# Layer-1 MLP of a two-layer decoder step: product 6 combined in PSUM, the small tokens' last products one step earlier

## The chip, the core and the metric

The kernel runs on one core of one Trainium2 chip. The metric is the device time of one execution in microseconds (us). The engines are named as the profile names them: PE (TensorE, matmuls), DVE (VectorE), ACT (ScalarE), POOL (GpSimd) and SP (the sync engine, whose queue issues most DMAs; POOL's queue issues those that add to what is already in a buffer). PSUM is where matmuls accumulate; one bank holds 128 x 512 fp32.

## The reference, cut to what matters

Each of two layers is a mixer and an MLP, with a layer norm behind each. The change lies in the MLP of layer 1, the last stage of the program. D_MODEL is 1024, D_FF 4096; there are 1024 prompt tokens, and 8 sample tokens (the "small tokens") that pass through the same weights.

```python
def post_norm(x, f, g, b):
    return layer_norm(DEEPNORM_ALPHA * x + f, g, b)

def sq_relu_mlp(x, w1, w2):
    h = jax.nn.relu(x @ w1)
    return (h * h) @ w2
...
        x_p = post_norm(x_p, sq_relu_mlp(x_p, mlp_w1[layer], mlp_w2[layer]), ln_mlp_g[layer], ln_mlp_b[layer])
        x_s = post_norm(x_s, sq_relu_mlp(x_s, mlp_w1[layer], mlp_w2[layer]), ln_mlp_g[layer], ln_mlp_b[layer])
    y_prompt = x_p[:, N_META:]
```

## The kernel before

`mlp1()` runs the hidden width in four groups (g = 0 to 3) of 1024. In a group, x times a 1024 x 1024 block of w1 (the "up" half) and the hidden block times a 1024 x 1024 block of w2 (the "down" half) are each done as 2 x 2 blocks with seven products instead of eight. The seven are numbered i = 1 to 7 and run in the order 1, 2, 5, 6, 4, 3, 7 (up) and 1, 5, 6, 3, 7, 4, 2 (down), in the last group 1, 5, 6, 7, 4, 3, 2. Their operands are sums and differences of quarter blocks, by the tables `UP_W`, `UP_X`, `DOWN_H`, `DOWN_W`.

**One product.** An operand is split into a high and a low part (`split` for what is on the chip: ACT casts in L202, DVE subtracts in L203; `weight_operand` for weights: ACT casts in L1621, POOL subtracts in L1622). `mm3` makes three matmuls (L206 to L208). A tile is 12 matmuls into one PSUM bank: eight tiles of 128 x 258 in an up product (512 prompt columns and 4 small-token columns for each half of the tokens), four of 128 x 512 in a down product. Tiles take banks in turn, three named `axt` and three named `mmt`, so a bank is wanted again six tiles later.

**After a tile.** `up_tile` adds the tile into the four result blocks c11, c12, c21, c22 of `HF`. In product 6 it makes c21 = tile - c12 (L1667, PSUM in, SBUF out) and then c22 = c22 + c21 (L1666, all SBUF); product 4 later adds its tile to c21. `hidden` applies the squared ReLU (L1655, L1656) and copies the small tokens' columns to `hs` (L1657). `chip_operand` also forms sums of blocks on DVE (L1596, into `RX`).

**Loads.** SP loads weights into a pool of five buffers `rw`, two buffers `raw`, and a four-part buffer `RW` for running sums (L1618); POOL's queue adds second terms to them by DMA (L1620). A load waits in SP's queue until its buffer is free, and all that is behind it waits too.

**The small tokens' down product.** `beside` makes four matmuls of 32 rows (L1642) into the accumulators `acc` for each quarter of w2, placed after the first tile of a chosen product. Where the product's own weights are that plain quarter, its buffers are used; otherwise four further loads are made (L1628), and their four `rw` buffers are held until those matmuls. In the last group these stand in down products 1 (plain), 5, 6 and 7.

**The end.** After down product 7 of the last group `samples_out` copies `acc` (L1559), transposes (L1564), reduces and normalizes the small tokens on DVE, with two matmuls between (L748, L754), transposes back (L1573) and writes `y_sample` (L1576). `normalize` and `last` finish each prompt tile: `bn_stats` (L1076), the root by POOL's pow (L1085), scaling, and the output, for tiles 2 and 3 by L1549 to L1551 at the very end, for the others by L1096, L1544 and an adding DMA (L1545) onto the bias rows that L1760 has put into `y_prompt` (3 MB).

A scheduler orders the instructions of each engine from the program's order; engines run their own instructions strictly in that order, and wait for each other by semaphores.

Of the kernel before, what the change touches and what calls it, by code (L numbers as in the profile page):

```python
# [21 lines left out]
P = 128  # L22
# [5 lines left out]
TS = 32  # L28
# [79 lines left out]
UP_W = {1: [(0, 0)], 2: [(0, 1)], 5: [(1, 0), (1, 1)], 6: ["run", (0, 0)], 4: [(1, 1)], 3: ["run", (0, 1)], 7: [(0, 0), (1, 0), "new"]}  # L108
UP_X = {1: [(0, 0)], 2: [(1, 0)], 5: [(0, 1), (0, 0)], 6: [(1, 1), "run"], 4: [(1, 0), "run"], 3: [(1, 1)], 7: [(0, 1), (1, 1)]}
DOWN_H = {1: [(0, 0)], 2: [(0, 1)], 5: [(1, 0), (1, 1)], 6: [(0, 0), "run"], 3: [(0, 1), "run"], 4: [(1, 1)], 7: [(1, 0), (0, 0)]}  # L110
DOWN_W = {1: [(0, 0)], 2: [(1, 0)], 5: [(0, 0), (0, 1)], 6: ["run", (1, 1)], 4: ["run", (1, 0)], 3: [(1, 1)], 7: [(1, 1), (0, 1), "new"]}
# [3 lines left out]
def hybrid_step(ctx, tc, A, dbg=None, upto=9):  # L115
    nc = tc.nc
    V, S, G, TE = nc.vector, nc.scalar, nc.gpsimd, nc.tensor
    dma = nc.sync.dma_start
# [224 lines left out]
    ps = smt()  # L343
# [16 lines left out]
    ps = smt()  # L360
# [202 lines left out]
    ps = smt()  # L563
# [4 lines left out]
    ps = smt()  # L568
# [8 lines left out]
    ps = smt()  # L577
# [15 lines left out]
    ps = smt()  # L593
# [20 lines left out]
    ps = smt()  # L614
# [986 lines left out]
    def weight_operand(terms, quarter, side=None):  # L1601

        hi, lo = (wsp.tile([P, 2048], F32R, name=n).rearrange("p (k n) -> p k n", n=512) for n in ("whi", "wlo"))
        run = terms[0] == "run"
        own = []

        def src(q, k):
            w, r0, c0 = quarter(*q)
            return w[r0 + k * P : r0 + (k + 1) * P, c0 : c0 + 512]

        for k in range(4):
            if run or (len(terms) > 1 and terms[-1] != "new"):
                t = RW[:, k, :]
            else:
                count[1] += 1
                t = wrp.tile([P, 512], F32, name="raw") if count[1] % 7 in (0, 3) else rawt()
            if not run:
                loads.append(dma(t, src(terms[0], k)).ins)  # L1618
            if len(terms) > 1:
                nc.gpsimd.dma_start(t, src(terms[1], k), accum_op=ALU.add)  # L1620
            S.copy(hi[:, k, :], t)  # L1621
            G.tensor_tensor(lo[:, k, :], t, hi[:, k, :].bitcast(F32), op=ALU.subtract)  # L1622
            own.append(t)
        if side:
            if terms != [side.quarter]:
                own = [rawt() for k in range(4)]
                for k in range(4):
                    dma(own[k], src(side.quarter, k))  # L1628
            sides.append((side, own))
        return hi, lo  # L1630

    w1, w2 = A["mlp_w1"][1], A["mlp_w2"][1]

    def operands(g, up, i):
        if up:
            left = weight_operand(UP_W[i], lambda h, k: (w1, 512 * k, 1024 * g + 512 * h))
            right = chip_operand(UP_X[i], lambda k, c: xr(c)[:, 4 * k : 4 * k + 4, :], TH, RX)
            return left, right

        def beside(k, t):  # L1640
            r, u = beside.quarter
            TE.matmul(acc[u][k * TS : (k + 1) * TS, :], hs[:, 4 * r + k, :], t, start=g == 0 and i in (1, 3), stop=g == 3 and r == 1)  # L1642


        beside.quarter = ({1: (0, 0), 3: (1, 1), 7: (0, 1), 2: (1, 0)} if g < 3 else {1: (0, 0), 5: (0, 1), 6: (1, 0), 7: (1, 1)}).get(i)
        left = chip_operand(DOWN_H[i], lambda c, k: HF[:, 4 * k : 4 * k + 4, c, :512], 512, XF[0][:, : 4 * TH] if g == 3 and i == 7 else RX)
        right = weight_operand(DOWN_W[i], lambda k, u: (w2, 1024 * g + 512 * k, 512 * u), beside if beside.quarter else None)
        return left, right

    ups = []  # L1650
# [8 lines left out]
    def up_tile(g, i, m, c, left, right, ps):  # L1659
        (ah, al), (bh, bl) = left, right  # L1660
        ps = ps[:, :CH]
        ms, cs = slice(m * P, (m + 1) * P), slice(c * CH, (c + 1) * CH)
        for k in range(4):
            mm3(ps, ah[:, k, ms], al[:, k, ms], bh[:, k, cs], bl[:, k, cs], k == 0, k == 3)
        c11, c12, c21, c22 = (HF[:, 4 * h + m, x, cs] for h in range(2) for x in range(2))
        add = lambda out, x, y: ups.append(V.tensor_tensor(out, x, y, op=ALU.add).ins)  # L1666
        less = lambda out, x, y: V.tensor_tensor(out, x, y, op=ALU.subtract)  # L1667
        if i == 1:
            S.copy(c12, ps)
        elif i == 2:  # L1670
            add(c11, c12, ps)
        elif i == 5:
            S.copy(c22, ps)
        elif i == 6:
            less(c21, ps, c12)
            add(c22, c22, c21)
        elif i == 4:
            add(c21, c21, ps)
        elif i == 3:
            less(c12, ps, c22)  # L1680
        else:
            add(c22, c22, ps)
            add(c21, c21, ps)
        if c:
            for h, x in {2: [(0, 0)], 3: [(0, 1)], 7: [(1, 1), (1, 0)]}.get(i, ()):
                hidden(h, x, m)
# [23 lines left out]
    def mlp1():  # L1710
# [6 lines left out]
        for at, (g, up, i) in enumerate(seq):  # L1717
# [14 lines left out]
            for t in range(4):  # L1732
                if t == 2:
                    nxt = operands(*seq[at + 1])
                if t == 1 and sides:
                    side, own = sides.pop(0)
                    for k in reversed(range(4)):
                        side(k, own[k])
                if up:
                    for c in range(2):  # L1740
# [9 lines left out]
                if g == 3:  # L1750
                    for c, u in {7: [(1, 1)], 4: [(1, 0)]}.get(i, ()):
                        yield 4 * c + t, u
            if g == 3 and not up and i == 7:
                samples_out()
            if g == 3 and up and i == 7:
                for x, nm in ((fg, "g"), (fb, "b")):
# [36 lines left out]
```

## Time and profile before

| | us |
|---|---|
| median of 3 runs | 2802.86 (2800.35 to 2804.12) |
| the profiled execution | 2807.25 |
| its span | 2805.4 |
| PE busy | 2725.4 (97%) |
| DVE busy | 1935.9 (69%) |
| ACT busy | 1107.1 (39%) |
| POOL busy | 1091.0 (39%) |

The span is from the first to the last instruction; 1.85 us of the profiled execution's time lie around it. PE is busy nearly throughout, so what counts is where it is not, and what is left after its last matmul. Times in the trace are from the span's start. The MLP of layer 1 is what runs from about 2110 us on.

### The profile page before, as it was taken

Reading aid. Unit: us, or ns where it says so; the run is one execution under the profiler, and the core shown is the slowest. Engines: PE = TensorE matmul, PEld = TensorE weight load, DVE = VectorE, ACT = ScalarE, POOL = GpSimd, SP = SyncE. Lnnn points to the kernel's source line nnn. Section 1 sums busy time; section 2 is a strip of 40 time slices with the busy share of each in tenths; the row PEclk is TensorE's granted clock in tenths of the full one; section 3 lists DMA queues with packets and bytes.
Section 4 is the critical chain, followed back from the end, with each engine's and each line's share of the span. In section 5 each row is a group of like instructions: output and inputs, shape, how many; then the busy total and the mean of one; then the engine's idle time right before and its main releaser. Section 6 shows DMA issues by size and latency. Waiting matters only on the chain.

```text
span 2805.4 us, 52242 instructions
## 1 busy us (share of the span) xinstructions
PE 2725.4 (97%) x19849; PEld 2237.5 (80%) x19849; DVE 1935.9 (69%) x3011; ACT 1107.1 (39%) x2266; POOL 1091.0 (39%) x744
## 2 busy tenths in 40 slices
PE   8989999999999999999999999899999999999997
PEld 5867767987777777777798989777899889798985
DVE  5375363678787787777667730887647888978698
ACT  4324463152221222221242112777526546355553
POOL 2132112234344443434234312200026667686765
PEclk9999999999999999999999999999999999999999
DMA  7475545735798898888658995212044555564674
GB/s 237 164 242 207 202 154 184 262 97 184 284 333 320 310 351 302 331 319 306 250 173 312 363 368 169 64 55 79 31 126 90 103 139 113 134 133 104 140 179 112
DMA packets 275624, 562.81 MB, mean 201 GB/s; under 512 B 23510, under 2 KB 144412, under 8 KB 271276
## 3 DMA queue, kind: packets, MB, share of 16 engines
q1 hardware_dynamic: 256076, 522.75, 54.0%
q0 software_dynamic: 19296, 36.71, 8.1%
q8 instruction: 156, 2.56, 0.4%
q14 instruction: 96, 0.79, 0.1%
HBM read 533.00 MB, written 29.52 MB: 201 GB/s over the span
## 4 chain that ended last, share of the span: by engine, by line
PE 78%; DVE 9%; DMA 4%; ACT 4%; issue 3%; POOL 1%; SPq 0%; DVEq 0%; POOLq 0%; ACTq 0%
PE mmt L206 18%; PE mmt L207 18%; PE mmt L208 18%; PE smt L983 4%; PE axt L206 3%; PE axt L208 3%; PE axt L207 3%; PE smt L1359 2%; ACT as L1337 1%; DMA swt<-in_mlp_w 1%; DVE pg L942 1%; PE prt L1333 1%; PE axt L1354 1%; DVE XH L203 1%; DVE sc L943 1%
## 5 line engine op out<-in xcount | busy, mean ns | idle before, releaser
L194 POOL TENSOR_TENSOR wlo<-raw,whi 128x512 fp32r<-128x512 f32 x252 | 361.5, 1448 | 719.0 <-ACT whi L193 616.2
L206 PE MATMUL mmt<-whi,XH 128*128 128x256 f32 (+1 forms) x1760 | 524.2, 300 | 1.1 <-DVE ast L1335 0.9
L207 PE MATMUL mmt<-wlo,XH 128*128 128x256 f32 (+1 forms) x1760 | 522.8, 298 | 0.6 <-POOL wlo L194 0.6
L206 PE MATMUL mmt<-XH,whi 128*128 128x512 f32 (+1 forms) x1216 | 435.9, 360 | 3.4 <-DVE HL L203 1.8
L208 PE MATMUL mmt<-whi,XL 128*128 128x256 f32 x1536 | 432.6, 285 | 0.0
L208 PE MATMUL mmt<-XH,wlo 128*128 128x512 f32 (+1 forms) x1216 | 432.4, 356 | 0.2 <-POOL wlo L1622 0.2
L193 ACT CAST whi<-raw 128x512 fp32r<-128x512 f32 x252 | 150.4, 619 | 574.2 <-DMA raw<-in_mlp_w 172.9
L206 PEld LDWEIGHTS mmt<-whi,XH 128*128 128x128 f32 x1760 | 330.8, 189 | 39.6 <-issue 24.3
L943 DVE TENSOR_REDUCE sc<-pg 128x16 f32<-128x1024 f32 x256 | 308.2, 1211 | 69.7 <-POOL pg L942 67.2
L207 PEld LDWEIGHTS mmt<-wlo,XH 128*128 128x128 f32 x1760 | 332.6, 189 | 16.8 <-issue 5.8
L942 DVE TENSOR_TENSOR pg<-pg,qb 128x1024 f32<-128x1024 f32 x192 | 267.1, 1398 | 63.5 <-DMA pg<-in_cache_k 50.5
L207 PE MATMUL mmt<-XL,whi 128*128 128x512 f32 x768 | 306.7, 400 | 0.0
L208 PEld LDWEIGHTS mmt<-whi,XL 128*128 128x128 f32 x1536 | 288.6, 189 | 7.3 <-issue 6.8
L206 PEld LDWEIGHTS mmt<-XH,whi 128*128 128x128 f32 x1216 | 229.6, 189 | 46.9 <-issue 7.6
L942 POOL TENSOR_TENSOR pg<-pg,qb 128x1024 f32<-128x1024 f32 x64 | 163.0, 2548 | 249.3 <-DMA pg<-in_cache_k 139.8
L208 PEld LDWEIGHTS mmt<-XH,wlo 128*128 128x128 f32 x1216 | 229.9, 189 | 36.1 <-issue 3.3
L206 PE MATMUL mmt<-whi,HH 128*128 128x512 f32 x512 | 204.8, 401 | 5.6 <-DVE Y L1172 3.7
L208 PE MATMUL mmt<-whi,HL 128*128 128x512 f32 x512 | 203.9, 398 | 0.0
L207 PE MATMUL mmt<-wlo,HH 128*128 128x512 f32 x512 | 203.4, 397 | 0.0
L1622 POOL TENSOR_TENSOR wlo<-rw,whi 128x512 fp32r<-128x512 f32 x92 | 154.4, 1737 | 93.6 <-ACT whi L1621 90.4
L1622 POOL TENSOR_TENSOR wlo<-RW,whi 128x512 fp32r<-128x512 f32 x96 | 164.1, 1750 | 59.1 <-ACT whi L1621 59.0
L207 PEld LDWEIGHTS mmt<-XL,whi 128*128 128x128 f32 x768 | 145.3, 189 | 39.3 <-issue 8.0
(438 smaller groups left out, 5697.6 us busy)
## 6 DMA issues: line engine op xcount, KB each, us to landing
pg<-in_cache_k SPq DMA_DIRECT2D x256, 512.0 KB
pg<-in_cache_v SPq DMA_DIRECT2D x256, 512.0 KB
raw<-in_mlp_w SPq DMA_DIRECT2D x164, 256.0 KB
swt<-in_mlp_w SPq DMA_DIRECT2D x32, 1024.0 KB
rw<-in_mlp_w SPq DMA_DIRECT2D x116, 256.0 KB
RW<-in_mlp_w POOLq DMA_DIRECT2D x96, 256.0 KB, 5.7
swt<-in_gla_w_in SPq DMA_DIRECT2D x12, 1024.0 KB
swt<-in_diff_w_in SPq DMA_DIRECT2D x12, 1024.0 KB
```

The costliest lines, as they stand in the source:

```text
L193: S.copy(hi[:, c], raw)
L194: G.tensor_tensor(lo[:, c], raw, hi[:, c].bitcast(F32), op=ALU.subtract)
L203: return eng.tensor_tensor(lo, src, hi.bitcast(F32), op=ALU.subtract)
L206: TE.matmul(ps, ah, bh, start=first, stop=False)
L207: TE.matmul(ps, ah, bl, start=False, stop=False)
L208: return TE.matmul(ps, al, bh, start=False, stop=last)
L942: eng.tensor_tensor(pg, pg, qb, op=ALU.mult)
L943: return V.tensor_reduce(sc[:, n, :], pg.rearrange("p (h d) -> p h d", d=64), op=ALU.add, axis=AX.X).ins
L983: m = TE.matmul(acc[i * TS : i * TS + 16, :256], w[r, n, :], pg[r, i * 256 : (i + 1) * 256], start=n == 0, stop=n == NPG).ins
L1333: TE.matmul(pss[m], qs[i][r, ts_], ks[j][r, x:y], start=i + j == 0, stop=i == 1)
L1359: TE.matmul(out, at, v, start=j == 0, stop=j == t + 1)
L1622: G.tensor_tensor(lo[:, k, :], t, hi[:, k, :].bitcast(F32), op=ALU.subtract)
```

## The change

Two edits. In `up_tile`, product 6 subtracts in place in the PSUM tile, adds that tile to c22, and copies it to c21: three DVE instructions with a PSUM operand for one with and one without. In the last group, the small tokens' quarters move: (0,1) from down product 5 to up product 7, (1,0) from 6 to 5, (1,1) from 7 to 6; and `samples_out` comes after down product 6 instead of 7. `beside` takes its place and quarter as arguments for that. The order in which the four matmuls use their buffers is unchanged in down products, and forward in the up product.

```diff
         if side:
-            if terms != [side.quarter]:
+            if not side.plain:
                 own = [rawt() for k in range(4)]
                 for k in range(4):
-                    dma(own[k], src(side.quarter, k))
+                    dma(own[k], side.block(k))
             sides.append((side, own))
...
+    def beside(g, r, u, plain):
+
+        def side(k, t):
+            TE.matmul(acc[u][k * TS : (k + 1) * TS, :], hs[:, 4 * r + k, :], t, start=g == 0 and r == u, stop=g == 3 and r == 1)
+
+        side.plain = plain
+        side.block = lambda k: w2[1024 * g + 512 * r + k * P : 1024 * g + 512 * r + (k + 1) * P, 512 * u : 512 * u + 512]
+        return side
+
     def operands(g, up, i):
+        if g < 3:
+            q = {} if up else {1: (0, 0), 3: (1, 1), 7: (0, 1), 2: (1, 0)}
+        else:
+            q = {7: (0, 1)} if up else {1: (0, 0), 5: (1, 0), 6: (1, 1)}
+        side = beside(g, *q[i], DOWN_W[i] == [q[i]] and not up) if i in q else None
         if up:
-            left = weight_operand(UP_W[i], lambda h, k: (w1, 512 * k, 1024 * g + 512 * h))
+            left = weight_operand(UP_W[i], lambda h, k: (w1, 512 * k, 1024 * g + 512 * h), side)
...
-        beside.quarter = ({1: (0, 0), 3: (1, 1), 7: (0, 1), 2: (1, 0)} if g < 3 else {1: (0, 0), 5: (0, 1), 6: (1, 0), 7: (1, 1)}).get(i)
...
         elif i == 6:
-            less(c21, ps, c12)
-            add(c22, c22, c21)
+            less(ps, ps, c12)
+            add(c22, c22, ps)
+            V.tensor_copy(c21, ps)
...
-                    for k in reversed(range(4)):
+                    for k in range(4) if up else reversed(range(4)):
                         side(k, own[k])
...
-            if g == 3 and not up and i == 7:
+            if g == 3 and not up and i == 6:
                 samples_out()
```

The scheduler's order follows. On DVE, in up product 6 of the first group, these rows stood before (tile 3's subtraction to tile 6's; `HF<-HF` is the addition to c22, `RX<-XR` a sum for a later operand, `XH` a low part):

```order
L1667 TENSOR_TENSOR HF<-axt,HF 128x258
L1666 TENSOR_TENSOR HF<-HF 128x258 x2
L1667 TENSOR_TENSOR HF<-mmt,HF 128x258
L1596 TENSOR_TENSOR RX<-XR_25159 128x1032
L1666 TENSOR_TENSOR HF<-HF 128x258
L1667 TENSOR_TENSOR HF<-axt,HF 128x258
L1666 TENSOR_TENSOR HF<-HF 128x258
L1667 TENSOR_TENSOR HF<-mmt,HF 128x258
```

and these stand there now, where the subtraction is L1674, the addition L1673 and the copy L1684:

```order
L1674 TENSOR_TENSOR axt<-axt,HF 128x258
L1673 TENSOR_TENSOR HF<-HF,axt 128x258
L1684 COPY HF<-axt 128x258
L1673 TENSOR_TENSOR HF<-HF,mmt 128x258
L1684 COPY HF<-mmt 128x258
L1674 TENSOR_TENSOR mmt<-mmt,HF 128x258
L1596 TENSOR_TENSOR RX<-XR_25159 128x1032
L1673 TENSOR_TENSOR HF<-HF,axt 128x258
L1684 COPY HF<-axt 128x258
L1674 TENSOR_TENSOR axt<-axt,HF 128x258
```

Every tile's bank is now read by three instructions, the last of them the copy.

On SP, around the bias rows for `y_prompt`, these DMAs stood before (`RW`: running sums; L1618: a product's own weights; L1628: the small tokens' weights; the bias rows are L1760):

```order
L1618 DMA RW<-in_mlp_w 128x512 x4
L1618 DMA rw<-in_mlp_w 128x512
L1760 DMA out_y_prompt<-in_ln_mlp_b 256x1024
L1760 DMA out_y_prompt<-in_ln_mlp_b 512x1024
L1628 DMA rw<-in_mlp_w 128x512 x2
L1618 DMA raw<-in_mlp_w 128x512
L1628 DMA rw<-in_mlp_w 128x512 x3
```

and these stand there now, with the bias rows as L1768:

```order
L1618 DMA RW<-in_mlp_w 128x512 x4
L1628 DMA rw<-in_mlp_w 128x512 x2
L1618 DMA rw<-in_mlp_w 128x512
L1618 DMA raw<-in_mlp_w 128x512
L1618 DMA rw<-in_mlp_w 128x512 x2
L1768 DMA out_y_prompt<-in_ln_mlp_b 256x1024
L1768 DMA out_y_prompt<-in_ln_mlp_b 512x1024
L1628 DMA rw<-in_mlp_w 128x512 x5
```

The small tokens' loads for up product 7 have come ahead, and the bias rows now stand behind two loads of down product 1 whose buffers PE frees in up product 7.

On DVE near the end, at the low part of down product 4's operand (`XH<-HF`), these rows stood before (`RP`: a running result):

```order
L203 TENSOR_TENSOR XH_24052<-HF,XH_86 128x1024
L1697 TENSOR_TENSOR RP<-mmt,RP 128x512
L203 TENSOR_TENSOR XH_24052<-HF,XH_86 128x1024
L1697 TENSOR_TENSOR Y<-Y,RP 128x512
L1697 TENSOR_TENSOR axt<-RP,axt 128x512
```

and these stand there now:

```order
L203 TENSOR_TENSOR XH_24052<-HF,XH_86 128x1024
L1705 TENSOR_TENSOR RP<-mmt,RP 128x512
L1566 TENSOR_REDUCE sz<-axt 128x4x8 x2
L203 TENSOR_TENSOR XH_24052<-HF,XH_86 128x1024
L1705 TENSOR_TENSOR Y<-Y,RP 128x512
L1568 SCALAR_TENSOR_TENSOR sz<-sx,sz 128x128 x2
L746 TENSOR_REDUCE ss1_31407<-sz 128x32
L1705 TENSOR_TENSOR axt<-RP,axt 128x512
```

The first steps of the small tokens' norm have moved up to here, behind the first of the two `XH<-HF`.

## Rows read from the trace of the kernel before

**Rows 1.** The end, a stretch: length, busy PE, PE load, DVE, ACT, POOL; clock, DMA share, GB/s

```profile
2746.00:2802.00 56.00, 44.92 (x199) 33.86 (x197) 55.88 (x100) 20.50 (x28) 31.00 (x26) 0.93 0.45 98
```

**Rows 2.** PE's waits from 2100 us on: for whom, total, times, longest

```profile
PE axt L206 <- DVE HF L1667: 4.1, 1, 4.1
```

**Rows 3.** PE in order of time (start, us): up 6, small-token matmuls, last prompt matmul

```profile
2167.45 0.28 PE L208 MATMUL mmt<-XH,wlo 128*128 128x258 f32 x1
2167.57 0.28 PE L206 MATMUL axt<-XH,whi 128*128 128x258 f32 x1
...
2716.08 1.05 PE L1642 MATMUL smt<-rw,hs 128*32 128x512 f32 x4
...
2790.18 0.40 PE L208 MATMUL mmt<-whi,XH 128*128 128x512 f32 x1
```

**Rows 4.** DVE in order of time: wait for an operand, last prompt tile, last outputs

```profile
2745.58 1.47 DVE L203 TENSOR_TENSOR XH<-HF,XH 128x1024 fp32r<-128x1024 f32 x1 [6.35 <-ACT XH L202]
...
2795.22 0.68 DVE L1697 TENSOR_TENSOR Y<-Y,mmt 128x512 f32<-128x512 f32 x1
...
2800.71 1.40 DVE L1550 SCALAR_TENSOR_TENSOR Y<-Y,brs,XR 128x512 f32<-128x512 f32 x2
```

**Rows 5.** The chain of waits behind down product 6's small-token matmuls: start, us

```profile
2731.03 1.12 PE smt L1642 x8
...
2732.46 4.56 DMA rw<-in_mlp_w
...
2737.54 6.41 DMA rw<-in_mlp_w
```

**Rows 6.** DVE in order of time, up product 6 of the first and last group

```profile
2165.81 1.65 DVE L203 TENSOR_TENSOR XH<-RX,XH 128x1032 fp32r<-128x1032 f32 x1
...
2167.72 2.61 DVE L1666 TENSOR_TENSOR HF<-HF 128x258 f32<-128x258 f32 x2
...
2170.59 1.22 DVE L1596 TENSOR_TENSOR RX<-XR 128x1032 f32<-128x1032 f32 x1
2171.73 5.42 DVE L1666 TENSOR_TENSOR HF<-HF 128x258 f32<-128x258 f32 x1
2177.08 0.41 DVE L1667 TENSOR_TENSOR HF<-axt,HF 128x258 f32<-128x258 f32 x1
...
2672.22 1.99 DVE L203 TENSOR_TENSOR XH<-XR,XH 128x1032 fp32r<-128x1032 f32 x1
```

**Rows 7.** POOL in order of time, the same two places

```profile
2171.01 0.88 POOL L1620 DMA_DIRECT2D rw<-in_mlp_w  x1 [0.96 <-PE mmt L208]
2171.62 5.24 POOL L1622 TENSOR_TENSOR wlo<-RW,whi 128x512 fp32r<-128x512 f32 x4
...
2668.95 6.41 POOL L1622 TENSOR_TENSOR wlo<-RW,whi 128x512 fp32r<-128x512 f32 x4 [2.93 <-ACT whi L1621]
```

**Rows 8.** Stretches of 1 us around PE's wait

```profile
2176.00:2177.00 1.00, 0.00 (x0) 0.00 (x0) 1.00 (x1) 0.00 (x0) 1.00 (x2) 0.52 0.79 258
...
2181.00:2182.00 1.00, 1.00 (x6) 1.00 (x6) 1.00 (x4) 0.00 (x0) 0.86 (x1) 0.50 1.07 166
...
2183.00:2184.00 1.00, 1.00 (x11) 1.00 (x10) 0.80 (x3) 0.00 (x0) 0.00 (x0) 1.00 1.16 182
```

**Rows 9.** DVE's groups by form from 2140 us on: busy us, mean ns, idle before

```profile
L1666 DVE TENSOR_TENSOR HF<-HF 128x258 f32<-128x258 f32 x32 | 34.9, 1101 | 0.2
L1666 DVE TENSOR_TENSOR HF<-HF,axt 128x258 f32<-128x258 f32 x64 | 25.2, 414 | 6.1 <-PE axt L208 6.0
```

**Rows 10.** SP's queue in order of time, last group

```profile
2682.71 1.29 SPq L1760 DMA_DIRECT2D out_y_prompt<-in_ln_mlp_b  x2
...
2687.09 0.33 SPq L1618 DMA_DIRECT2D raw<-in_mlp_w  x1
...
2706.28 1.31 SPq L1628 DMA_DIRECT2D rw<-in_mlp_w  x3
```

**Rows 11.** POOL, when the raw load of 2687.09 has landed

```profile
2704.77 0.88 POOL L1620 DMA_DIRECT2D raw<-in_mlp_w  x1 [5.29 <-DMA raw<-in_mlp_w]
```

More of the change, by code (lines that the diff above doesn't have):

```diff
@@ L1632, in hybrid_step @@
     w1, w2 = A["mlp_w1"][1], A["mlp_w2"][1]
-    def operands(g, up, i):
+    def beside(g, r, u, plain):
[4 more added lines that the diff above has]
+        return side
+    def operands(g, up, i):
+        if g < 3:
[3 more added lines that the diff above has]
+        side = beside(g, *q[i], DOWN_W[i] == [q[i]] and not up) if i in q else None
         if up:
-            left = weight_operand(UP_W[i], lambda h, k: (w1, 512 * k, 1024 * g + 512 * h))
+            left = weight_operand(UP_W[i], lambda h, k: (w1, 512 * k, 1024 * g + 512 * h), side)
             right = chip_operand(UP_X[i], lambda k, c: xr(c)[:, 4 * k : 4 * k + 4, :], TH, RX)
             return left, right
-        def beside(k, t):
-            r, u = beside.quarter
-            TE.matmul(acc[u][k * TS : (k + 1) * TS, :], hs[:, 4 * r + k, :], t, start=g == 0 and i in (1, 3), stop=g == 3 and r == 1)
-        beside.quarter = ({1: (0, 0), 3: (1, 1), 7: (0, 1), 2: (1, 0)} if g < 3 else {1: (0, 0), 5: (0, 1), 6: (1, 0), 7: (1, 1)}).get(i)
         left = chip_operand(DOWN_H[i], lambda c, k: HF[:, 4 * k : 4 * k + 4, c, :512], 512, XF[0][:, : 4 * TH] if g == 3 and i == 7 else RX)
-        right = weight_operand(DOWN_W[i], lambda k, u: (w2, 1024 * g + 512 * k, 512 * u), beside if beside.quarter else None)
+        right = weight_operand(DOWN_W[i], lambda k, u: (w2, 1024 * g + 512 * k, 512 * u), side)
         return left, right
```

## The prediction

> **What bounds the kernel now.** I read the share of busy time first, then PE's waits over the last stage, then PE and DVE in order of time where a wait or the end lies, and last the queues behind those places. PE is 97% busy over the span, so a change outside PE is worth only what PE waits for it, and what is left after PE's last matmul. From 2100 us on the longest wait of PE is one of 4.1 us, for DVE, on a bank that L1667 had not yet read [rows 2]. After it there is none of that size until the small tokens' own tail. The end is different: the last prompt matmul starts at 2790.18 and takes 0.40 [rows 3], but DVE is busy for 55.88 of the 56 us from 2746 to 2802 [rows 1], adds the last tile's product at 2795.22 and begins its last two steps at 2800.71 [rows 4]. So the last 56 us are DVE's, and PE's matmuls there have some 4.6 us of room (2795.22 less 2790.58). DVE enters this stretch at 2745.58, after 6.35 us of waiting for an operand's cast [rows 4]; that cast waits behind weights whose buffers PE frees in down product 6: its small-token matmuls at 2731.03, a load of 4.56, an adding load of 6.41 [rows 5].
>
> **Product 6, first group: the wait that goes.** Here lies the one stall. DVE's all-SBUF addition began at 2171.73 and lasted 5.42 us; the subtraction that frees PE's next bank stood behind it and ran at 2177.08 for 0.41 [rows 6]. Over the same time POOL did four subtractions in 5.24, about 1.31 each, straight after a DMA issue at 2171.01 [rows 7]. PE did nothing in the stretch of 2176 to 2177, and then ran at the lower clock (0.50 granted, 1.2 GHz) at 2181 and at full clock again by 2183 [rows 8]. From 2177.5, when that subtraction ends, to about 2182.6 is 5.1 us at half speed, which is 2.55 lost. With the 4.1 of the wait, this place costs 6.6.
>
> The Trainium skill ("SBUF — State Buffer", Who interferes with whom) says that a DVE instruction with both inputs in SBUF contends with a GpSimd one that reads SBUF, that one with at most one SBUF input does not, and that whoever came first holds on for its whole instruction. The trace agrees as to the forms (the rows below), but 5.42 us is longer than any one POOL instruction here; it was held over four of them. By the page alone a blocked instruction would wait at most one POOL instruction, 1.3, and the sum below would come out some 0.4 lower, an estimate.
>
> In the changed kernel none of product 6's instructions has both inputs in SBUF. The addition with a PSUM input took 414 ns in the mean over 64, the all-SBUF one 1101 over 32 [rows 9]. So the two forms are told apart by the same line and size, and I take 0.42 for each of the three new instructions; the copy isn't in the trace, so it is bounded by 0.41 (the PSUM additions) from below and 1.10 from above, taken at 0.42, since it too reads PSUM. DVE's work in product 6 goes from 32 x (0.42 + 1.10) = 48.6 to 32 x 3 x 0.42 = 40.3 us over four groups, but this time lies beside PE and is worth nothing by itself.
>
> The Trainium skill ("VectorE: DVE Perf Modes", Rules for kernel authors) advises as few instructions in a chain as can be, which speaks against 32 added copies, an estimate of 13 us of DVE time. The row of 1101 ns decides against it here, where the instruction replaced costs more than the two that stand for it.
>
> **What takes the wait's place.** A bank is now free only after the third instruction. PE starts a matmul every 0.12 us (2167.45 and 2167.57, where a new tile begins) [rows 3], so a tile is 1.44 and the sixth tile after comes 8.6 later; DVE's three steps are 1.25 a tile, which leaves little for anything else between. The order has L203 and then three tiles' worth of work ahead of the first copy: L203 ends at 2165.81 + 1.65 = 2167.46 [rows 6], then the third subtraction, an addition and the copy at some 0.34 from start to start, so the first bank comes free at about 2168.5, where PE wanted it at 2167.57: 0.9 of waiting. Of the later ones only the copy behind the next L203 is in danger. That L203 now stands four tiles earlier than before, and begins while POOL's run until 2176.86 [rows 7] goes on; it takes 1.65 alone, and what PE then waits is 0.4 if it gets through, 2.0 if it is held until the run's end. I take 1.2, near the middle, since both have a row on their side. So 2.1 comes back and this place gives 6.6 - 2.1 = 4.5. Its bounds are 6.6 (no wait comes) and about 0 (some other all-SBUF instruction, L203 or L1596, takes the block over for as long as L1666 did).
>
> **Product 6, the other groups.** PE had no such wait in them [rows 2], so nothing can be gained. One copy stands behind an L203 there too. In the last group that L203 took 1.99 at 2672.22 while POOL ran from 2668.95 to 2675.36 [rows 6, 7]. Held to the end of that run it would last 3.1, 1.2 more, with PE's slack there some 0.5 to 1.2 by my estimate from tiles of 1.44. I take 0, because the row shows it getting through; the bound is 1.4 a group, 4.2 in all.
>
> **The small tokens' matmuls, last group.** Four matmuls in up product 7 come and four in down product 7 go, 1.05 us a set [rows 3], so PE does the same work. Their four loads move from down 7 to up 7. What moves with them on SP is the 3 MB of bias rows, issued at 2682.71 before [rows 10]. These were costly to what followed: a load issued at 2687.09 [rows 10] was waited for until 2704.77 [rows 11], 17.7 us. Now they stand behind two loads whose buffers PE frees only in up product 7, so I expect them at about 2694.5 (12 us later, a tile row of up 7 further on), and the same 22 us of full queues then reaches to 2716. Down product 5's small-token loads were issued at 2706.28 for matmuls at 2716.08 [rows 3, 10]; these matmuls now come at about 2717.1, the four of up 7 being before them. If the loads land within 9 us PE waits for nothing; if they take 10.8, 0 to 2.5. I take +1.0. The bound above is a landing as late as that of the raw load: 2706.5 + 17.7 = 2724.2 to 2724.5, a wait of 7.4, and, as after the wait in product 6, 2.5 more at the lower clock, 9.9.
>
> **The end.** Since DVE carries the end, what counts is when it gets its operand (2745.58 before) and how much it then has to do. The sample steps move up, but the first of them stands behind the first `XH<-HF` of that place, so the same instructions remain after it: nothing gained there. The four matmuls moved before it put down 6's small-token matmuls 1.0 later, and with them the loads of [rows 5]; four loads fewer stand ahead of down 7's own, for which I take back 0.5. So +0.5. The bounds are -4.6, if DVE lost so much work ahead of the last tile that PE's room vanished, and +4, if as many as three of the moved DVE steps met POOL as L1666 did (3 x 1.3).
>
> **The sum**, against the profiled execution's 2807.25: -4.5 + 0 + 1.0 + 0.5 = -3.0, so 2804.2. That execution is 4.4 above the median of 2802.86; the same -3.0 on the median gives 2799.9.
>
> **The rivals.** (A) *The wait goes whole, and nothing comes in its place.* L203 gets through POOL's run, the first copy is in time as tiles start later, the bias rows hurt nobody, and DVE's shorter product 6 leaves it 1 to 2 us ahead at the end: -6.6 - 1.4 = -8, 2794.8. For it: the PSUM forms' 414 ns hold in 64 cases. Against it: three steps of 0.42 against tiles of 1.44 leave no room for an L203 between.
> (B) *The later bias rows starve down product 5.* Its small-token loads land as the raw load did, PE waits 7.4 and loses 2.5 to the clock: -4.5 + 9.9 + 0.5 = +5.9, 2808.8, slower. It decides from the point where those loads take over 10 us from issue to landing; at 13.5 the gain of product 6 is half gone, above that all of it goes. For it: the 17.7 us. Against it: that load was issued 4 us behind the bias rows, these come some 12 behind.
> (C) *The block finds another instruction.* POOL's run of four is still there, and L203 or L1596, both all-SBUF, stand in it: PE waits as before, and the rest gives +1.5: 2804.4. For it: L203 is moved into the run's last third. Against it: the 1.99 in the last group.
>
> **How the numbers follow.** 0.2%, about 5.6 us, is what a measurement here can tell from no change: faster is below 2797.3, slower above 2808.5. I give the forecast 0.50, A 0.27, C 0.13 and B 0.10. A lies mostly on the faster side, and a little of the forecast's lower edge joins it: 0.29 faster. C and nearly all the forecast are within: 0.63. B, which straddles the limit, and the sum of several upper bounds give 0.08 slower. The range is 2794.0 to 2807.0: below, A's own value and a little more; above, C with the other groups' bound of part, short of B.
>
> **What would show it.** In the changed profile, three instructions of about 0.41 for each tile of product 6 and no L1673 over 0.5 show the first step right; PE's list of waits without the 4.1, and the clock at 1.00 from 2176 to 2183, show what it is worth. A wait of PE's `axt` or `mmt` on the copy (L1684) of 0.9 and another behind L203 would show the price. PE's wait of L1642 for `rw` in down 5, and how long after issue those loads land, decide on B; an L203 or L1596 above 4 us in product 6 decides on C. For the end, DVE's first `XH<-HF` against 2745.58, and the last add against PE's last matmul. I am wrong if PE's wait in product 6 stays at 3 us or more, if down 5 waits above 3, or if DVE's last stretch is shorter by more than 2.

## The result: slower

The changed kernel takes 2810.73 us (median of eight runs, 2805.62 to 2814.67) where the kernel before takes 2801.61 (eight runs): a ratio of 1.0037, 95% interval 1.0024 to 1.0049. Run again on two other occasions it gave 1.0030 (1.0015 to 1.0046) and 1.0013 (0.9997 to 1.0030). The forecast was 2799.9, the range ended at 2807. The profiled execution has a span of 2808.9 against 2805.4; its MLP began 3.4 us earlier than in the profile of before (2122.87 against 2126.23 for the first addition of product 2), so the MLP itself lost 6.9.

PE's waits from 2100 us on in the changed kernel (for whom, total, times, longest), beside [rows 2]:

```profile
PE axt L206 <- DVE HF L1684: 6.2, 1, 6.2
PE smt L748 <- DVE ss L746: 2.7, 1, 2.7
```

The wait in product 6 has grown, and is now for the copy. The second wait is new, at a place of which the prediction did not speak: a matmul of the small tokens' norm.

**Product 6.** DVE of the changed kernel in order of time (start, us), beside [rows 6]:

```profile
2157.82 8.64 DVE L203 TENSOR_TENSOR XH<-RX,XH 128x1032 fp32r<-128x1032 f32 x1 [3.79 <-ACT XH L202]
2166.49 1.23 DVE L1596 TENSOR_TENSOR RX<-XR 128x1032 f32<-128x1032 f32 x1
2167.64 0.43 DVE L1674 TENSOR_TENSOR axt<-axt,HF 128x258 f32<-128x258 f32 x1
2167.98 0.42 DVE L1674 TENSOR_TENSOR mmt<-mmt,HF 128x258 f32<-128x258 f32 x1
2168.31 1.22 DVE L203 TENSOR_TENSOR XH<-RX,XH 128x1032 fp32r<-128x1032 f32 x1
2169.45 0.43 DVE L1674 TENSOR_TENSOR axt<-axt,HF 128x258 f32<-128x258 f32 x1
2169.79 0.42 DVE L1673 TENSOR_TENSOR HF<-HF,axt 128x258 f32<-128x258 f32 x1
2170.12 0.42 DVE L1684 COPY HF<-axt 128x258 f32<-128x258 f32 x1
```

POOL over the same time, beside [rows 7]:

```profile
2156.99 1.57 POOL L1622 TENSOR_TENSOR wlo<-RW,whi 128x512 fp32r<-128x512 f32 x1
...
2158.85 1.89 POOL L1622 TENSOR_TENSOR wlo<-rw,whi 128x512 fp32r<-128x512 f32 x1
2160.10 1.48 POOL L1620 DMA_DIRECT2D RW<-in_mlp_w  x1
2160.72 2.19 POOL L1622 TENSOR_TENSOR wlo<-raw,whi 128x512 fp32r<-128x512 f32 x1
2161.98 3.38 POOL L1622 TENSOR_TENSOR wlo<-rw,whi 128x512 fp32r<-128x512 f32 x2
2167.50 0.89 POOL L1620 DMA_DIRECT2D rw<-in_mlp_w  x1 [2.14 <-DMA rw<-in_mlp_w]
```

The all-SBUF `L203` that stands ahead of product 6's steps in DVE's order (it makes the next product's operand, product 4's) takes 8.64 us where its like takes 1.22 (the row of 2168.31). It ends at 2166.46, 1.1 after POOL's run ends at 2165.36: it got through only when POOL stopped. Such time beyond an instruction's own length, spent beside POOL's subtractions, is called a hold below. Seven more instructions follow on DVE, the last of them the copy that frees the first bank, at 2170.54. Then the clock (stretches of 2 us; the third number from the end is the granted clock, beside [rows 8]):

```profile
2166.00:2168.00 2.00, 0.00 (x0) 0.00 (x0) 1.97 (x4) 0.00 (x0) 0.50 (x1) 1.00 0.84 282
...
2172.00:2174.00 2.00, 2.00 (x12) 2.00 (x11) 2.00 (x6) 0.00 (x0) 0.00 (x0) 0.50 0.00 0
...
2178.00:2180.00 2.00, 2.00 (x19) 2.00 (x18) 2.00 (x4) 1.13 (x2) 2.00 (x1) 1.00 0.37 114
```

The forms themselves cost what was forecast (DVE's groups by form: busy, mean ns, idle before; beside [rows 9]):

```profile
L1673 DVE TENSOR_TENSOR HF<-HF,axt 128x258 f32<-128x258 f32 x80 | 31.8, 414 | 8.5 <-PE axt L208 8.4
...
L1684 DVE COPY HF<-axt 128x258 f32<-128x258 f32 x16 | 6.6, 415 | 0.0
```

**The sample output.** DVE, then POOL, then PE of the changed kernel at the new place of the small tokens' norm:

```profile
2751.16 2.63 DVE L1568 SCALAR_TENSOR_TENSOR sz<-sx,sz 128x128 f32<-128x128 f32 x2
2753.82 0.58 DVE L746 TENSOR_REDUCE ss<-sz 128x32 f32<-128x256 f32 x1
```

```profile
2747.14 6.50 POOL L1622 TENSOR_TENSOR wlo<-RW,whi 128x512 fp32r<-128x512 f32 x4 [1.12 <-ACT whi L1621]
```

```profile
2754.46 0.41 PE L748 MATMUL smt<-ss,c_inv 128*128 128x32 f32 x2 [2.74 <-DVE ss L746]
2754.70 0.48 PE L208 MATMUL mmt<-whi,XH 128*128 128x512 f32 x1
```

In the kernel before, the same two `L1568` stand later in DVE's order and take 0.48 together:

```profile
2764.28 0.48 DVE L1568 SCALAR_TENSOR_TENSOR sz<-sx,sz 128x128 f32<-128x128 f32 x2
```

So again an all-SBUF step is held beside POOL's run; it ends 0.15 after the run (2753.64). Two engines lose by it: DVE itself, and PE, with prompt matmuls queued behind `L748`. The chain of work that ended last goes through DVE here (start, us):

```profile
2749.53 1.71 DVE Y L1705
2751.24 2.56 DVE sz L1568 x2
...
2753.82 0.58 DVE ss L746
2754.40 0.62 DVE axt L1705
```

From there it stays on DVE to the end, but for 0.6 us on POOL; PE's wait is not on it.

### The profile page after: what moved, and what is told of

Same layout as the page of the kernel before. It is cut to its first block, busy times and chain, and to the rows that moved or that the text cites. A ratio compares the mean times of both kernels' runs of the same rounds, so it can differ in the third digit from the quotient of the medians.

```text
span 2808.9 us, 52278 instructions
## 1 busy us (share of the span) xinstructions
PE 2721.8 (97%) x19849; PEld 2235.5 (80%) x19849; DVE 1927.8 (69%) x3043; ACT 1107.7 (39%) x2266; POOL 1086.2 (39%) x744
## 4 chain that ended last, share of the span: by engine, by line
PE 81%; DVE 8%; ACT 4%; DMA 3%; issue 3%; POOL 1%; SPq 0%; DVEq 0%; POOLq 0%; ACTq 0%
PE mmt L206 19%; PE mmt L207 18%; PE mmt L208 18%; PE smt L983 4%; PE axt L206 3%; PE axt L208 3%; PE axt L207 3%; PE smt L1359 2%; ACT as L1337 1%; DVE XH L203 1%; PE prt L1333 1%; DVE pg L942 1%; PE smt L712 1%; PE axt L1354 1%; PE smt L723 1%
## 5 line engine op out<-in xcount | busy, mean ns | idle before, releaser
L942 DVE TENSOR_TENSOR pg<-pg,qb 128x1024 f32<-128x1024 f32 x192 | 256.6, 1343 | 63.8 <-DMA pg<-in_cache_k 51.5
```

The costliest lines, as they stand in the source:

```text
L942: eng.tensor_tensor(pg, pg, qb, op=ALU.mult)
```

## The experiments

To compare executions whose earlier stages differ by several us, each profile is cut in three. The **first stretch** goes from product 2's first addition of an `mmt` tile to the first small-token matmul of the first group (before: 2126.23 to 2214.49, 88.26 us); the **middle** from there to DVE's first `XH<-HF` of down product 4 in the last group (2745.58, 531.09); the **last** from there to the span's end (59.82; the span is printed to 0.1 us, so the last stretch is good to that). Ratios are against the runs of before on the same chip.

**Each edit alone, and two variants.** `p6_only` has product 6 as changed and all else as before; `side_only` the rest of the change; `side_keep7` is `side_only` with

```diff
-            if g == 3 and not up and i == 6:
+            if g == 3 and not up and i == 7:
                 samples_out()
```

and `p5_pre` is the kernel before with

```diff
         elif i == 5:
-            S.copy(c22, ps)
+            less(c22, ps, c12)
         elif i == 6:
             less(c21, ps, c12)
-            add(c22, c22, c21)
+            add(c22, c22, ps)
```

> Product 6's three-instruction form alone, the small tokens as in the kernel before; in the first group every engine's order is that of the changed kernel, in the last group that of the kernel before, but for product 6. Theory: this form makes the first group's product 6 dearer by about 2.3 us, because a bank is now held until the copy and an all-SBUF operand step (L203) ahead of it, held by POOL, delays all of it: PE waits 5 to 6.5 us there for the copy, L203 of 7 us or more, and the kernel comes to about 2804 beside 2801.6 (+1 to +4). Rival: the 8.64 us of L203 in the changed profile was one execution's chance; then L203 takes 1.2 to 2, PE's wait there is under 2 us, and the kernel is 3 to 5 us faster than before.

Measured: 1.0005 (0.9988 to 1.0021); `L203` 8.72, PE's wait 6.2, first stretch 90.73. The hold came as the theory says; the time is too uncertain to tell.

> The small tokens' move alone, product 6 as before. Theory: the sample tokens' norm now has two matmuls (L748, L754) in the middle of PE's work, and PE waits for DVE at the first 2 to 3.5 us and 0.5 at the second; with the later end of the outputs +4 to +7, about 2807. PE's wait of 4.1 us on L1667 in the first group is as before. Rival: the loss of the changed kernel lies all in product 6; then this is within 2 us of before.

Measured: 1.0010 (0.9995 to 1.0025); the wait at `L748` 2.7, last stretch 62.45. The time, some 2.8 us, is below the theory's. PE's wait in product 6 was 0.9, not 4.1, though the order there is that of before: the first sign that the hold is chance.

> As the run with the small tokens' move alone, but the sample output stays after down product 7 as before. Theory: PE's wait for L746 goes, and what is left is the move of the loads and matmuls: 0 to +2 us against before, 3 to 5 us less than with the output moved. Rival: the bias rows' place or the loads cost, not the output; then it is as slow as the run with the output moved.

Measured: 1.0009 (0.9994 to 1.0024); no wait at `L748`, last stretch 60.59, 1.9 less than in `side_only`. The 3 to 5 us expected between the two do not show in the times. Product 6, in the order of before, showed this on DVE:

```profile
2154.21 8.75 DVE L203 TENSOR_TENSOR XH<-RX,XH 128x1032 fp32r<-128x1032 f32 x1 [3.69 <-ACT XH L202]
2163.00 1.23 DVE L1596 TENSOR_TENSOR RX<-XR 128x1032 f32<-128x1032 f32 x1
2164.15 0.42 DVE L1674 TENSOR_TENSOR HF<-axt,HF 128x258 f32<-128x258 f32 x1
```

and PE's waits this:

```profile
PE axt L206 <- DVE HF L1674: 3.7, 1, 3.7
```

The same `L203` is held as long with the old form. But there the first bank comes free 1.6 us after it (2164.57 less 2162.96), in the new form 4.1 (2170.54 less 2166.46): 2.5 us, the difference of the two waits.

> The kernel before with another way round the all-SBUF additions: product 5 puts (tile - c12) into c22 on DVE where ACT copied the tile, and product 6 writes c21 = tile - c12 and adds the tile to c22, so two instructions with a PSUM operand each, no copy behind which the bank waits for a third. Theory: the 4.1 us wait and most of the 2.5 at the lower clock go, 3 to 6.6 us faster, about 2796. Rival: the hold by POOL falls on another all-SBUF instruction (L203, L1596) in the same place, and the time is within 2 us of before or above it.

Measured: 1.0016 (1.0003 to 1.0029), `L203` held 9.77, PE's wait 5.5: the rival. Taking SBUF operands out of product 6 did nothing about the hold of an instruction ahead of it.

**Without the holds.** (The `L203` that is held makes product 4's operand; where an expectation below calls it product 6's, that instruction is meant.) `low_dve_old` is before, and `low_dve_p6` is `p6_only`, with POOL's run ahead of product 6 taken away:

```diff
-            G.tensor_tensor(lo[:, k, :], t, hi[:, k, :].bitcast(F32), op=ALU.subtract)
+            (eng or G).tensor_tensor(lo[:, k, :], t, hi[:, k, :].bitcast(F32), op=ALU.subtract)
...
-            left = weight_operand(UP_W[i], lambda h, k: (w1, 512 * k, 1024 * g + 512 * h))
+            left = weight_operand(UP_W[i], lambda h, k: (w1, 512 * k, 1024 * g + 512 * h), eng=V if (g, i) == (0, 4) else None)
```

`sum_psum` is the changed kernel with the small tokens' sum in PSUM, and `p6_keep7` the changed kernel with the sample output behind down product 7:

```diff
-            V.tensor_reduce(zc, pt.rearrange("p (j k t) -> p j t k", j=4, k=4)[:, :, 0:NS, :], op=ALU.add, axis=AX.X)
-            zc = z[:, 4 * u : 4 * u + 4, :]
-            V.scalar_tensor_tensor(zc, sx[:, 4 * u : 4 * u + 4, :], ALPHA, zc, ALU.mult, ALU.add)
+            r0 = smt()[:, : 4 * NS].rearrange("p (j t) -> p j t", j=4)
+            V.tensor_reduce(r0, pt.rearrange("p (j k t) -> p j t k", j=4, k=4)[:, :, 0:NS, :], op=ALU.add, axis=AX.X)
+            V.scalar_tensor_tensor(zc, sx[:, 4 * u : 4 * u + 4, NM : NM + NS], ALPHA, r0, ALU.mult, ALU.add)
```

> The kernel before, with one thing changed: the low part of product 4's weights in the first group (four subtractions of 128x512, L1622) is made by DVE instead of POOL, so that POOL has no run of subtractions while DVE makes product 6's operand (L203). Theory: the hold of DVE there comes from that run; without it L203 takes 1.2 to 1.7, PE waits for no bank (under 1 us), the clock stays at 1.00, and the stretch from the first addition of product 2 to the first small-token matmul of the first group is 81 to 84 us (83.7 to 88.3 in the three profiles with this product 6 so far); the whole 2 to 5 us faster than before. Rival: the hold has to do with POOL's DMA issues or with the loads, not its subtractions; then L203 or another all-SBUF instruction is again held for 4 us or more and the stretch is 86 or more.

Measured: 1.0003 (0.9987 to 1.0018), first stretch 81.55, no wait of PE for a DVE instruction there. DVE:

```profile
2166.68 1.94 DVE L203 TENSOR_TENSOR XH<-RX,XH 128x1032 fp32r<-128x1032 f32 x1 [3.71 <-ACT XH L202]
```

and POOL, whose last subtraction ends at 2167.50, with two DMA issues behind it:

```profile
2165.93 1.57 POOL L1622 TENSOR_TENSOR wlo<-RW,whi 128x512 fp32r<-128x512 f32 x1
2167.18 2.08 POOL L1620 DMA_DIRECT2D RW<-in_mlp_w  x2
```

`L203` ends 1.1 us after the last subtraction, beside the issues. So it is the subtractions that hold it, and the rival falls. The stretch's gain is not seen in the time.

> The same on the kernel with product 6's three instructions alone. Theory: the copy costs only behind a hold, since a held DVE must then do six instructions before the first bank comes free, where the old form needs one; without the hold PE waits under 1.5 us and the stretch is 82 to 85 us (90.6 and 90.7 with POOL's run), within 1.5 us of the run with the old product 6. Rival: three instructions a bank are too much for DVE in any case; PE waits 3 us or more for the copy and the stretch stays 4 us or more above that of the old product 6.

Measured: 1.0008 (0.9989 to 1.0026), first stretch 83.91, PE's wait for the copy in it 2.0. The stretch is as expected, but 2.4 above `low_dve_old`, and the wait is over the 1.5 expected. Part of this may come from the four subtractions that DVE now makes at this place, which the run does not separate; the rival is partly right. Three more waits for the copy, 2.2 together, come in the third group, behind a low part of the weights for which PE had waited 1.6.

> The changed kernel, with the small tokens' sum (L1566) written to PSUM, so that L1568 reads one operand from PSUM; every engine's order is kept but for one place. Theory: L1568's 2.63 us in the changed profile is a hold by POOL's run of subtractions, which an instruction with a PSUM operand escapes: it takes under 0.4 each, PE's wait of 2.7 at L748 falls to 0.7 or less, and the end comes 2 to 3 us sooner than the changed kernel's. Rival: PE waits at L748 for DVE's other work (the two L203 and the additions ahead); then the wait stays above 2.

Measured: DVE at the sample output and PE's waits there:

```profile
2749.88 0.27 DVE L1568 SCALAR_TENSOR_TENSOR sz<-sx,smt 128x32 f32<-128x32 f32 x2
2750.19 0.59 DVE L746 TENSOR_REDUCE ss<-sz 128x32 f32<-128x256 f32 x1
```

```profile
PE smt L748 <- DVE ss L746: 0.5, 1, 0.5
```

POOL's run is still there (6.48 from 2745.86), `L1568` goes through it in 0.27, and the last stretch is 59.85 where the changed kernel has 63.27. (`L1568` is a quarter as wide here; but the full width took only 0.48 in the kernel before.) That part of the loss is shown in the profile. The time was 1.0027 (1.0008 to 1.0045), not clearly below the changed kernel's. DVE's last instructions, first in the changed kernel, then here:

```profile
2802.45 1.41 DVE L1550 SCALAR_TENSOR_TENSOR Y<-Y,brs,XR 128x512 f32<-128x512 f32 x2
```

```profile
2797.81 1.41 DVE L1550 SCALAR_TENSOR_TENSOR Y<-Y,brs,XR 128x512 f32<-128x512 f32 x2
```

From the first `XH<-HF` to their end it is 58.2 and 54.9, and 56.5 in the kernel before [rows 4]. So without the hold DVE is done 1.7 sooner than before. The last stretch is no shorter for it, since 4.9 us follow DVE's end where 3.3 did.

> The changed kernel with the sample output back behind down product 7. Theory: the first stretch is 90 to 91 us as in the other two kernels with three instructions; no wait at L748; PE's last matmul some 43 us after DVE has its operand for down product 4 (46.9 in the changed kernel), and 3 to 5 us faster than the changed kernel, that is +3 to +6 against before. Rival: the loss lies in the loads of the small tokens' quarters; then it is as slow as the changed kernel.

Measured: 1.0015 (0.9997 to 1.0033); no wait at `L748`, last stretch 60.30; but the first stretch 82.97, not 90 to 91, with `L203` at 1.63: no hold this time. The time, some 4.2 us, is within the theory's.

**What is chance.** `after_again` and `before_again` are the two kernels once more; `side_psum` is `sum_psum` with the old product 6.

> The changed kernel once more. Question: how much of the first result (+0.37%, eight runs a side) is chance, and whether L203's hold of 8.64 us in product 6 comes every time. Theory: the hold comes in some executions and not in others (2 of 4 so far with this product 6, where the instruction order up to there is the same), so the stretch from product 2's first addition to the first small-token matmul is either near 83 or near 90.6 us; the wait of 2.5 to 3 us at L748 is always there; the time is +4 to +7 us against before, less than the first result's +9.1. Rival: the hold belongs to the changed kernel; the stretch is 90 to 91 again and the time +8 to +11.

Measured: 1.0030 (1.0015 to 1.0046), first stretch 82.99, `L203` 1.63, PE's wait for the copy 0.8; the wait at `L748` 2.6, and this time the clock fell behind it (below). The stretch is one of the theory's two; the time, some 8.4 us, is the rival's. POOL and DVE where `L203` was held in the first profile of this kernel:

```profile
2162.39 1.59 POOL L1622 TENSOR_TENSOR wlo<-RW,whi 128x512 fp32r<-128x512 f32 x1
```

```profile
2163.45 1.63 DVE L203 TENSOR_TENSOR XH<-RX,XH 128x1032 fp32r<-128x1032 f32 x1 [4.03 <-ACT XH L202]
```

and the stretches behind `L748`:

```profile
2750.00:2752.00 2.00, 0.00 (x0) 0.00 (x0) 1.97 (x3) 0.00 (x0) 1.53 (x2) 0.99 0.00 0
...
2754.00:2758.00 4.00, 4.00 (x10) 3.09 (x10) 4.00 (x8) 2.03 (x3) 0.00 (x0) 0.50 0.00 0
2758.00:2760.00 2.00, 2.00 (x8) 1.60 (x7) 2.00 (x4) 2.00 (x5) 1.34 (x2) 0.81 0.01 4
```

> The kernel before once more, against itself: what the comparison tells from no change, and a second profile of its first group. Theory (chance): L203 at 35 us after product 2's first addition or the L1666 of 10 us later is held for some other length than in the first profile (1.7 and 5.4), the stretch lies anywhere from 82 to 89 us; the ratio is within 0.15% of 1. Rival: the first profile's picture (L203 1.71, L1666 5.42, PE's wait 4.1) comes again to within 0.3 us.

Measured: 0.9995 (0.9980 to 1.0010), first stretch 87.11, and on DVE, in the kernel whose first profile had 1.71 there:

```profile
2160.40 9.01 DVE L203 TENSOR_TENSOR XH<-RX,XH 128x1032 fp32r<-128x1032 f32 x1 [3.44 <-ACT XH L202]
```

So the hold comes and goes from execution to execution, in both kernels, and the 5.42 us of `L1666` in the first profile was one of its shapes.

> Product 6 as before; the small tokens' quarters and their output moved; and their sum written to PSUM. Theory: with the hold of L1568 gone, PE waits under 0.7 at L748 and does not fall to the lower clock as it did in the run with the move alone (granted 0.66 from 2750 to 2760 there): DVE's operand for down product 4 to PE's last matmul 43 to 44.5 us (49.1 there), and the kernel within 2 us of before. Rival: the loads and the bias rows cost as well: PE waits 2 us or more for the small tokens' weights in down 5, and the kernel is 3 us or more slower than before.

Measured: 1.0010 (0.9996 to 1.0024); the wait at `L748` 0.5, operand to last matmul 43.99, last stretch 58.86; PE waited 1.5 for the small tokens' weights in down 5. The time, some 2.8 us, lies between the theory and the rival.

**Are the two holds the whole loss?** `low_after`, `low_sum_psum` and `low_side_psum` are the changed kernel, `sum_psum` and `side_psum` with product 4's low part on DVE; `p6_twice` is `p6_only` with `V.tensor_copy(c21, ps)` twice.

> The changed kernel with the low part of product 4's weights in the first group made by DVE, so that the hold ahead of product 6 cannot come. Theory: the stretch from product 2's first addition to the first small-token matmul is 82.5 to 84.5 us, the wait of 2.6 at L748 stays, and the kernel is +3 to +6 us against before (+9 with the hold in some of its executions). Rival: holds in product 6 explain little of the loss; the time stays at +8 to +10.

Measured: 1.0052 (1.0033 to 1.0070), first stretch 85.38, the wait at `L748` 2.4. The time is at the rival's, but three instructions beside the four subtractions make PE wait 2.0 for the copy here too, and 2.2 more come in the third group, as in `low_dve_p6`; so this run does not isolate the hold.

> The changed kernel with both holds taken away: product 4's low part by DVE, the small tokens' sum in PSUM. Theory: the two holds are the loss; what is left is within 2.5 us of before (the loads of the small tokens in down 5 still cost about 1). Rival: something that the two places do not show (the other groups' product 6, the bias rows) costs as much; the time is +5 us or more.

Measured: 1.0014 (1.0001 to 1.0027), first stretch 85.40, last 59.42. Next to `low_after` it differs by the sum in PSUM alone, and the two intervals do not meet: 0.38%, some 10 us, more than the 2 to 4 that the profiles show at that place. The middle stretches of these two profiles differ as well, 536.80 against 531.07, so not all of it need be the sum. Against before it is some 3.9 us, between the theory and the rival.

> The same with product 6 as before, the version with neither hold nor copy. Theory: 0 to 4 us faster than before, the first stretch 81.5 to 83 us, the last from DVE's operand for down product 4 to the end 59 to 60 us (59.4 to 59.8 before, 62.4 to 63.3 with the output moved and the sum in SBUF). Rival: the moved loads cost more than the holds give; no faster than before.

Measured: 1.0008 (0.9990 to 1.0025), first stretch 81.57, last 59.52: no faster than before, the rival. No version tried beats the kernel before.

> Product 6's three instructions alone, with the copy made twice: a bank is held for four instructions. Theory: without a hold DVE keeps up with PE only just (1.25 us a tile and 1.44 for PE), so a fourth instruction (1.65 a tile) makes PE wait in every group: 2 to 3 us for the eight tiles of a product in the later groups too, 5 to 12 us slower than before in all, and 92 us or more for the first stretch in an execution with the hold. Rival: only held executions are slowed; the later groups show no wait and the time is within 3 us of the single copy's.

Measured: 1.0058 (1.0038 to 1.0079); PE's waits:

```profile
PE axt L206 <- DVE HF L1678: 6.4, 1, 6.4
...
PE mmt L206 <- DVE HF L1678: 2.9, 3, 1.0
```

With a fourth instruction each of the three later groups gains a wait of 1.0. Of the ten profiles with three instructions eight show none there, and two the 2.2 in the third group named above. The third instruction is the last that fits. The time, some 16 us, is above the 5 to 12 expected; where the rest goes was not followed.

**Do the shares add up?** Both edits and each alone, on one chip (`f_both`, `f_side`, `f_p6`).

> The changed kernel, beside its two edits alone, all on one chip with the same runs of before, for the shares of the two. Theory: the shares add up; both +8 to +11 us, product 6 alone +2 to +5, the small tokens' move alone +4 to +7. Rival: the two make each other dearer (each alone within 3 us of before, both together +8 or more).

Measured: 1.0013 (0.9997 to 1.0030); first stretch 84.89, the wait at `L748` 2.5, last stretch 63.85. That is some 3.6 us, below the +8 to +11 expected, and does not bear out the rival either.

> The small tokens' move alone, in the comparison with both. Theory: +4 to +7 us, most of it the wait of 2.6 us at L748 and the lower clock behind it; DVE's operand for down product 4 to the end 62 to 64 us. Rival: within 3 us of before.

Measured: 1.0025 (1.0010 to 1.0040), some 7 us; the wait 2.7, last stretch 61.61. The upper end of the theory.

> Product 6's three instructions alone, in the comparison with both. Theory: +2 to +5 us in the mean; in the profile either the hold (first stretch 90.6 us) or none (83). Rival: within 2 us of before, since the hold strikes the old form as often.

Measured: 1.0009 (0.9993 to 1.0025); no hold, first stretch 82.98, PE's wait for the copy 0.8. Nothing rules out that the edits simply add: product 6 alone +0.05 and +0.09%, the small tokens alone +0.10 and +0.25%, both together +0.37, +0.30 and +0.13%.

## Why the prediction was wrong

The first stretch in the thirteen profiles that have POOL's run and either form of product 6, by the length of `L203`, which begins some 35 us into it:

| length of `L203` | old product 6 | three instructions |
|---|---|---|
| 1.6 to 1.8, no long hold | 82.69; 88.26 (the first profile, `L1666` held 5.42) | 82.90, 82.97, 82.98, 82.99 |
| 4.3 | 83.74 | 84.89 |
| 8.6 to 9.0 | 87.11, 87.12, 87.18 | 90.57, 90.73 |
| mean | 86.0 | 85.4 |

- **"The wait that goes" was sized from one execution, and is the term that failed by most (3.9 us).** The 6.6 us were the price of a hold that takes turns among the all-SBUF instructions beside POOL's runs: of the six profiles of the old form only the first has it on `L1666` for 5.42, and four have it on `L203`, ahead of product 6. With no long hold at all the two forms are alike (82.9 to 83.0 against 82.69); there the forecast's first copy, 0.9 late, was 0.8 late, and the second wait, put at 1.2, did not come. With `L203` held for 8.6 or more the new form is 3.5 worse, as its first bank waits for a third instruction behind others. Over six and seven executions the edit is worth 0.6 us in the mean, within a spread of some 3 in either form, not 4.5. The rival with the block at another instruction (C, 0.13) was the right one, but even it put the block at the later `L203`, and no worse than before.
- **"The end: nothing gained" took the moved steps at nothing, and failed too.** DVE does carry the end, as the prediction says; but two of the steps moved up, the `L1568`, now stand beside POOL's run and take 2.63 where they took 0.48. The bound of +4 had this case (moved steps that meet POOL), and the sum had nothing for it. The norm's matmuls `L748` and `L754` were not followed into PE's order either: PE waits for `L746`, 2.4 to 2.7 in all six profiles with the early output and the sum in SBUF, and in five of them runs at the lower clock behind it. But in four of the six (`after`, `f_both`, `f_side`, `low_after`) the chain that ended last stays on DVE there; only in `side_only` and `after_again` does it go through PE's slow matmuls. The last stretch is 58.7 to 60.3 (mean 59.6, eight profiles) with the quarters and the output in their old places, 61.6 to 63.9 (mean 62.6, six) with the changed ones, and 58.9 to 59.9 (mean 59.4, four) with the sum in PSUM: +2.9 where 0 stood, and none of it once the hold of `L1568` is gone. That is a balance of two: without the hold the early output has DVE done 1.4 sooner than before (54.9 after the first `XH<-HF` against 56.3, in the mean), but what follows DVE's end, 3.3 to 3.8 before, is now 4.0 to 4.9. POOL's last adding output (`L1545`), issued some 6.5 before DVE's end in the kernel before and in the changed one, took 5.8 to land in the first and 7.9 in the second, that is till 1.3 after DVE's end. That this is what lengthens the tail, and why it lands later, was not tested.
- **The small tokens' loads: right.** The bias rows were put at 2694.5 and came at 2694.23; the down 5 matmuls at 2717.1, and came at 2717.43. The wait there was taken at 1.0: the twelve profiles with the move show 0 to 2.2, 1.0 in the mean. Rival B did not come. The middle stretch is 533.5 in the mean of these twelve (530.6 to 538.0) against 531.2 in seven without the move (529.1 to 534.8; `p6_twice` aside), +2.3, of which 1.05 are the four matmuls moved into it. The prediction has +1.5 there: 1.0 for the loads, and the 0.5 by which DVE was to get its operand later.
- **Product 6 in the other groups: right at 0 in most executions**, with less room than thought, as `p6_twice` shows. In five profiles a low part of the weights came 1.6 late in the third group; behind it PE waited 1.2 for the old form and 2.2 for the new one.
- **The sum.** From the stretches: -0.6 + 2.3 + 2.9 = +4.6, against -4.5 + 1.5 + 0 = -3.0. The times give +3.6 to +10.4 for the same kernel on three occasions. The mean ratios go the way of the stretches: 1.0004 with the small tokens unmoved (five runs, `p5_pre` and `p6_twice` aside), 1.0012 with the move and the output behind product 7 (two), 1.0015 with the early output and its sum in PSUM (four), 1.0028 with the early output as changed (six); a single ratio is uncertain by some 0.0015. What lies between +4.6 and the times of the changed kernel is not settled: the profiles are a few executions, and how often the hold comes in the timed runs can't be seen in them.

With one operand from PSUM `L1568` takes 0.27 in the middle of POOL's run, with two from SBUF 2.63. The Trainium skill ("SBUF — State Buffer", Who interferes with whom) says that a DVE instruction with at most one SBUF input, outside the two-port modes, does not contend with GpSimd. The trace agrees. `L203` was held for 9.0 us across five POOL subtractions of 1.6 to 2.2, and in other executions of the same code only for the rest of the one that it began beside. The Trainium skill (the same section) says that whoever issues first gets the shared ports for the whole instruction, a sentence that it writes of DVE's two-port modes; it fits the short waits, and did not tell the length of the long ones.

## What to carry to other kernels

A long instruction in one profile may be a hold that falls elsewhere in the next execution; take a second profile before pricing its removal, and ask which instructions of the same kind stand ahead of it. Each further instruction between a matmul's end and its bank's release costs little (0.8 us of waiting here) until something ahead of them is late, and then it costs in full (2.5 more). When a step of one engine is moved earlier, look at what the other engines do at the new place: two instructions of 0.48 us together took 2.63 there, on the engine that carries the end, and a matmul of 0.4 us that waits for their result held all matmuls behind it.

## What was not expected of the hardware

In all twenty profiles the `L203` ahead of product 6 began during a POOL subtraction and ended 1.1 us after the end of one. In six of the fifteen with POOL's run it was the subtraction that `L203` began beside, in three the next one, in six the last of the run, with `L203` at 8.6 to 9.8 us; in the five profiles where DVE makes product 4's low part, so that no further subtraction of POOL follows, it was the first. What goes with the outcome is how late in that first subtraction `L203` began: 0.52 to 0.69 us before its end in the six that got through, 0.75 to 1.87 in the nine that did not. Why a waiting DVE is passed over by POOL's next subtraction is not shown. PE's wait of 2.7 at `L748` was followed by full clock in the first profile of the changed kernel and by the lower one (0.50) in the five others.
